# Second parts of weights on GpSimd during the expert choice, expert lists of 80 and 48 rows

## The chip, the cores and the metric

The kernel runs on one core of a Trainium2 chip. The metric is the device time of one execution in microseconds. The kernel before took 1815.71 us (median of three runs, 1813.82 to 1818.97).

## What is computed

Two encoder layers over 256 tokens of width 1024, all in float32. A layer is a mixer (one input projection, a neighbourhood attention, a sliding-window attention, gates, an output projection) and then a feed-forward part with retrieved experts, which is where the change lies:

```python
def peer_ffn(x, w_query, sub_keys, expert_down, expert_up):
    def chunk(xc):                                   # 128 tokens
        q = (xc @ w_query).reshape(PEER_CHUNK, PEER_HEADS, 2, half)
        s = jnp.einsum('thpk,pnk->thpn', q, sub_keys)
        sv, si = lax.top_k(s, PEER_TOPK)             # 16 of 128, twice a head
        cand = (sv[:, :, 0, :, None] + sv[:, :, 1, None, :]).reshape(...)
        cidx = (si[:, :, 0, :, None] * 128 + si[:, :, 1, None, :]).reshape(...)
        top_s, sel = lax.top_k(cand, PEER_TOPK)      # 16 of 256 pairs
        eidx = jnp.take_along_axis(cidx, sel, axis=-1)
        g = jax.nn.softmax(top_s, axis=-1)
        u, vv = expert_down[eidx], expert_up[eidx]   # 16384 experts
        act = gelu(jnp.einsum('td,thkd->thk', xc, u))
        return jnp.einsum('thk,thkd->td', (g * act), vv)
```

## The kernel before

**Number format.** Every float32 product is made of three matmuls: a weight is split into a first part `wh` (ScalarE, line 198) and a second part `wl = raw - wh` (VectorE, line 201), the left side likewise, and TensorE adds `h*h`, `h*l` and `l*h`. A unit of weights is 128 x 1024 values, 512 KB. The class `Stream` (lines 154 to 225) loads units on SyncE's queue some units ahead, splits them and hands them to TensorE; `splits` lists the names of the subtractions, in order.

**Stages of a layer.** Mixer; query projection, 16 units in four groups; then the *down stage*, 128 units: TensorE multiplies all 16384 rows of `peer_down` with all 256 tokens (lines 1363 to 1365, 24 matmuls a unit), and the result, after the gelu (line 1307), is `act`, 128 partitions x 128 rows i of experts x 256 tokens. Beside these matmuls runs the *expert choice*: scores (line 944), top 16 in eight groups n = 0 to 7 (`topk_lane`, lines 916 to 924 and the additions of line 964, all VectorE), indices and softmax (`index_lane`), and then 76 *gate groups* a layer (`gate_group`, lines 1065 to 1109), which multiply the gates into `act` in two passes: 44 groups for the rows 0 to 79 and 32 for the rows 80 to 127. A pass also counts which experts are used at all.

**Lists.** When a pass is through, `rank_lane` gives each expert of its list a place: first those that only the tokens of chunk 0 use, then those of both chunks, then those of chunk 1 alone. `send_lane` scatters the rows of `act` to these places in DRAM (line 1208, one indirect DMA a row of 128 experts, from GpSimd's queue). The *up stage* then reads a list back in blocks of 128 experts (line 1239, SyncE's queue), fetches the rows of `peer_up` that these experts name (line 1268, an indirect DMA of 512 KB from GpSimd's queue), splits them as units and multiplies (line 1397): a block costs six matmuls of 512 columns for each chunk that uses it. A list is a tuple (first row, rows, cap, ea, sb): the blocks sb to ea-1 are made for both chunks, 0 to sb-1 for chunk 0 alone, ea to cap-1 for chunk 1 alone. `WHOLE` names rows that are not sorted at all: their 128 experts are taken as they stand, for both chunks, their units loaded by plain DMAs on SyncE's queue, between the first list and the second. What the caps leave out would be made up by `make_up` behind a branch.

**Order and pace.** The order of instructions on each engine is fixed when the program is written out: `Lanes` keeps planned clocks (p TensorE, v VectorE, s ScalarE) and lets side lanes issue when their turn has come by planned costs. Waits between engines come from the data. A sending lane first needs its list's places (`lane_need([("rank", r)])`), then for each row that row's gelu and gates. Between sends it keeps a pace counted in weight splits: the counter starts three behind the splits written so far, each send adds 0.4 (first list) or, in the second list, 1.8 and later 0.6, and the send waits in the program and on the chip for the split that the counter names. The second list also waits until ten units of the up stage are loaded:

```python
            whole = up0 + len([x for x in seq if x[1] == 0])
            while r and st.nd < up0 + DEEP:
                yield None
            pace = len(st.splits) - 3.0
                pace += 0.4 if r == 0 else 1.8 if st.nd < whole else 0.6
```

`st.nd` counts the units loaded, `up0` is the first unit of the up stage. The reading back of a list starts only when all its rows are sent (line 1239 behind `sent`). Four units are loaded ahead; from the fourth unit before the up stage on, `st.depth` is ten, so that the split of the first up unit, written out two units before the end of the down stage, asks for units up to ten ahead.

Of the kernel before, what the change touches and what calls it, by code (L numbers as in the profile page):

```python
# [10 lines left out]
F32 = mybir.dt.float32  # L11
# [37 lines left out]

LISTS = [(0, 80, 66, 49, 16), (88, 40, 33, 25, 8)]  # L50
WHOLE = (80, 8)

# [18 lines left out]
class Lanes:  # L71
# [8 lines left out]
    def __init__(self):  # L80
        self.clk = {"p": 0.0, "v": 0.0, "s": 0.0}
        self.lanes = []
        self.stuck = 0
        self.urgent = 0
# [71 lines left out]
class Stream:  # L156


    def __init__(self, nc, pool, srcs, lanes):
        self.nc, self.pool, self.srcs, self.lanes = nc, pool, srcs, lanes  # L160
        self.raw, self.parts, self.ready = {}, {}, {}
        self.nd = self.np = self.want = 0
        self.ahead = self.depth = AHEAD
        self.busy, self.pooled, self.splits = set(), [], []
        self.rows = None
# [24 lines left out]
    def _prep(self, u):  # L190
        self.load(u)
        while u not in self.raw:
            yield None
            self.load(u)
        yield ("s", 0.97)
        r = self.raw.pop(u)
        h = self.pool.tile([128, UNIT], F32R, name="wh", bufs=AHEAD)
        self.nc.scalar.activation(h, r, AF.Copy)  # L198
        self.ready[u] = (yield ("v", 1.14)) - 0.05
        lo = self.pool.tile([128, UNIT], F32R, name="wl", bufs=AHEAD)  # L200
        self.splits.append(self.nc.vector.tensor_sub(lo, r, h.bitcast(F32)).ins.name)  # L201
        self.parts[u] = (h, lo)
        self.busy.discard(u)
        self.load(u + self.depth)
# [19 lines left out]
def encoder_kernel(ctx, tc, x_in, wts, downs, ups, gains, gate_bias, qk_norm, rpb, sink, skeys, consts, sums, out,  # L224
# [244 lines left out]
    u = 0  # L469
    acc_first = None  # L470

    for l in range(depth):
# [474 lines left out]
        def topk_lane():  # L947
            for n in range(8):
                cg, ch = n // 2, n % 2
                yield from lane_need([("s", cg, ch)])  # L950
                sc = area(4096 + n * 512, 512).rearrange("p (q n) -> p q n", n=128)
                s2 = area(8192 + (n % 2) * 512, 512).rearrange("p (q n) -> p q n", n=128)
# [238 lines left out]
        def send_lane(r):  # L1191

            i0, w = LISTS[r][:2]
            yield from lane_need([("rank", r)])
            whole = up0 + len([x for x in seq if x[1] == 0])
            while r and st.nd < up0 + DEEP:
                yield None
            pace = len(st.splits) - 3.0
            for i in range(i0, i0 + w):
# [17 lines left out]

                pace += 0.4 if r == 0 else 1.8 if st.nd < whole else 0.6
                sends[r].append(snd.ins)
# [350 lines left out]
```

## Time and profile before

| | us |
|---|---|
| median of the runs | 1815.71 |
| the profiled execution | 1816.92 |
| its span | 1815.1 |
| TensorE busy | 1777.3 (98%) |
| VectorE busy | 1452.2 (80%) |
| ScalarE busy | 1085.9 (60%) |
| GpSimd busy | 495.4 (27%) |

Both layers do the same work, the second some 901 us after the first. Times of a stage below are those of the first layer in the profiled execution; a busy TensorE means that a matmul was under way, and where matmuls are issued every 0.12 us (256 columns) or 0.23 us (512 columns) without a gap nothing holds TensorE back.

### The profile page before, as it was taken

To read this page: it belongs to the slowest core of one execution; us is meant where nothing else is said; L and a number is where in the kernel's file an instruction comes from. 1 tells how busy PE (TensorE), PEld (TensorE's weight loads), DVE (VectorE), ACT (ScalarE), POOL (GpSimd) and SP (SyncE) were. 2 spreads that over 40 slices of the span, in tenths; PEclk is the share of its full clock that TensorE was granted. 3 is DMA by queue.
4 is the path that set the end of the run, shared out by engine and by line. 5 is a ranking of instruction groups with operands and counts; after the bars stand their busy time and mean duration, and the time that the engine had idled before them with its cause. 6 is when DMAs were issued, how large, how long until landed. Compare 5 with 4: busy or idle time off the path is not lost. (4 is left out here: it accounts for less than half of the span.)

```text
span 1815.1 us, 38007 instructions
## 1 busy us (share of the span) xinstructions
PE 1777.3 (98%) x14646; PEld 1637.2 (90%) x14646; DVE 1452.2 (80%) x3270; ACT 1085.9 (60%) x1792; POOL 495.4 (27%) x448
## 2 busy tenths in 40 slices
PE   8999999999999989999999999999999999999998
PEld 7889899999999988878788998999999999888786
DVE  6986798988987877766689778989888878777665
ACT  5675555566656656665646654555665567566654
POOL 0000000000008767775200000000000187777661
PEclk9999999999999999999999999999999999999999
DMA  7535455544446869989564355555444478799893
GB/s 262 159 112 171 150 171 180 184 152 152 152 143 233 245 217 353 328 316 347 192 214 143 107 164 165 172 180 183 150 153 150 152 234 249 239 341 332 297 344 130
DMA packets 130519, 377.42 MB, mean 208 GB/s; under 512 B 17552, under 2 KB 43792, under 8 KB 130320
## 3 DMA queue, kind: packets, MB, share of 16 engines
q1 hardware_dynamic: 90288, 239.28, 42.5%
q0 software_dynamic: 40032, 135.54, 20.4%
q8 instruction: 119, 1.95, 0.4%
q14 instruction: 80, 0.66, 0.1%
HBM read 342.00 MB, written 32.75 MB: 206 GB/s over the span
## 5 line engine op out<-in xcount | busy, mean ns | idle before, releaser
L201 DVE TENSOR_TENSOR wl<-raw,wh 128x1024 fp32r<-128x1024 f32 x476 | 579.6, 1221 | 157.0 <-ACT wh L198 148.9
L198 ACT ACTIVATE wh<-raw 128x1024 fp32r<-128x1024 f32 x476 | 503.0, 1058 | 249.9 <-PE bank L1364 61.1
L1363 PE MATMUL bank<-TT,wh 128*128 128x256 f32 x2048 | 591.7, 289 | 0.0
L1364 PE MATMUL bank<-TT,wh 128*128 128x256 f32 x2048 | 578.9, 283 | 0.0
L1365 PE MATMUL bank<-TT,wl 128*128 128x256 f32 x2048 | 578.4, 282 | 0.0
L1364 PEld LDWEIGHTS bank<-TT,wh 128*128 128x128 f32 x2048 | 392.0, 191 | 0.0
L1365 PEld LDWEIGHTS bank<-TT,wl 128*128 128x128 f32 x2048 | 391.8, 191 | 0.0
L1363 PEld LDWEIGHTS bank<-TT,wh 128*128 128x128 f32 x2048 | 391.4, 191 | 0.0
L1397 PE MATMUL bank<-wh,TT 128*128 128x512 f32 x1296 | 350.2, 390 | 6.2 <-DVE TT L1286 2.2
L1208 POOL DMA_INDIRECT rows<-act,rank x240 | 280.4, 1168 | 96.3 <-issue 60.9
L1397 PEld LDWEIGHTS bank<-wh,TT 128*128 128x128 f32 x1296 | 242.2, 188 | 62.2 <-DVE TT L1286 5.4
L885 POOL IOTA act<- 128x128 uint32 (+2 forms) x6 | 2.0, 332 | 1081.1 <-PE bank L365 410.7
L201 DVE TENSOR_TENSOR wl<-act,wh 128x1024 fp32r<-128x1024 f32 x126 | 154.3, 1226 | 75.9 <-ACT wh L198 75.9
L1397 PE MATMUL bank<-wl,TT 128*128 128x512 f32 x648 | 200.6, 389 | 1.5 <-issue 1.5
L198 ACT ACTIVATE wh<-act 128x1024 fp32r<-128x1024 f32 x126 | 133.5, 1061 | 96.2 <-PE bank L1397 84.6
L1268 POOL DMA_INDIRECT act<-in_ups_dram,act x118 | 126.6, 1073 | 71.3 <-issue 30.2
L1397 PEld LDWEIGHTS bank<-wl,TT 128*128 128x128 f32 x648 | 121.6, 188 | 25.4
L445 PE MATMUL bank<-TT,wh 128*128 128x256 f32 x448 | 130.1, 290 | 1.6 <-ACT raw_ka L574 1.0
L447 PE MATMUL bank<-TT,wh 128*128 128x256 f32 x448 | 126.6, 283 | 0.0
L448 PE MATMUL bank<-TT,wl 128*128 128x256 f32 x448 | 126.6, 283 | 0.0
L1307 ACT ACTIVATE act<-bank 128x256 f32<-128x256 f32 (+9 forms) x216 | 66.1, 350 | 84.7 <-PE bank L1365 82.2
L1109 DVE TENSOR_TENSOR act<-act,bank 128x480 f32<-128x480 f32 (+32 forms) x152 | 71.3, 471 | 51.8 <-ACT act L1105 45.8
(267 smaller groups left out, 2852.1 us busy)
## 6 DMA issues: line engine op xcount, KB each, us to landing
raw<-in_downs_dram SPq DMA_DIRECT2D x256, 512.0 KB, 3.8
raw<-in_wts_dram SPq DMA_DIRECT2D x132, 512.0 KB, 4.2
act<-rows SPq DMA_DIRECT2D x100, 129.0 KB, 5.9
act<-rows SPq DMA_DIRECT2D x98, 64.5 KB, 5.2
act<-in_ups_dram SPq DMA_DIRECT2D x8, 512.0 KB, 8.9
raw<-in_ups_dram SPq DMA_DIRECT2D x8, 512.0 KB, 9.8
rows<-act,rank POOLq DMA_INDIRECT x240
act<-in_ups_dram,act POOLq DMA_INDIRECT x118
```

The costliest lines, as they stand in the source:

```text
L198: self.nc.scalar.activation(h, r, AF.Copy)
L201: self.splits.append(self.nc.vector.tensor_sub(lo, r, h.bitcast(F32)).ins.name)
L445: nc.tensor.matmul(o, wh, rh, start=first and i == 0 and pc == 0, stop=False, skip_group_check=True)
L447: nc.tensor.matmul(o, wh, rl, start=False, stop=False, skip_group_check=True)
L448: nc.tensor.matmul(o, wl, rh, start=False, stop=last and i == len(kcs) - 1 and pc == 1, skip_group_check=True)
L1109: nc.vector.tensor_mul(a, a, bv[:, 0:g])
L1208: snd = nc.gpsimd.indirect_dma_start(byrank[r], bass.IndirectOffsetOnAxis(ap=rank[:, i:i + 1], axis=0), afl[:, i * ROW:(i + 1) * ROW], None)
L1268: nc.gpsimd.indirect_dma_start(w, None, ups_rows, bass.IndirectOffsetOnAxis(ap=num, axis=0), element_offset=l * 16384 * D)
L1363: nc.tensor.matmul(o, lh, TT[:, :, 0, kc, :], start=kc == 0, stop=False)
L1364: nc.tensor.matmul(o, lh, TT[:, :, 1, kc, :], start=False, stop=False)
L1365: nc.tensor.matmul(o, ll, TT[:, :, 0, kc, :], start=False, stop=kc == 7)
L1397: nc.tensor.matmul(oacc[ch][hf], a, r[:, hf * 512:(hf + 1) * 512], start=first[hf] and a is lh and r is h, stop=last and a is ll)
```

## The change

Three edits. The lists become 80 and 48 rows: the second list takes over the eight rows that were whole, and its caps go from (33, 25, 8) to (40, 29, 9). While `topk_lane` is in its groups 0 to 6, the second part of each weight unit is subtracted by GpSimd instead of VectorE, with a planned clock g of its own. And the second list no longer waits for ten loaded up units: it is sent as soon as its places are known, behind the first list, at 0.4 a send until six up units are loaded and at 1.8 from there on.

```diff
-LISTS = [(0, 80, 66, 49, 16), (88, 40, 33, 25, 8)]
-WHOLE = (80, 8)
+LISTS = [(0, 80, 66, 49, 16), (80, 48, 40, 29, 9)]
+WHOLE = (80, 0)
...
-        self.clk = {"p": 0.0, "v": 0.0, "s": 0.0}
+        self.clk = {"p": 0.0, "v": 0.0, "s": 0.0, "g": 0.0}
...
+        self.gpsimd = False
...
         self.nc.scalar.activation(h, r, AF.Copy)
-        self.ready[u] = (yield ("v", 1.14)) - 0.05
+        engine, req = ((self.nc.vector, ("v", 1.14)), (self.nc.gpsimd, ("g", 2.5)))[self.gpsimd]
+        t = yield req
         lo = self.pool.tile([128, UNIT], F32R, name="wl", bufs=AHEAD)
-        self.splits.append(self.nc.vector.tensor_sub(lo, r, h.bitcast(F32)).ins.name)
+        self.splits.append(engine.tensor_sub(lo, r, h.bitcast(F32)).ins.name)
+        self.ready[u] = t - 0.05
...
                 yield from lane_need([("s", cg, ch)])
+                st.gpsimd = n < 7
...
             yield from lane_need([("rank", r)])
-            whole = up0 + len([x for x in seq if x[1] == 0])
-            while r and st.nd < up0 + DEEP:
-                yield None
             pace = len(st.splits) - 3.0
...
-                pace += 0.4 if r == 0 else 1.8 if st.nd < whole else 0.6
+                pace += 0.4 if r == 0 or st.nd < up0 + 6 else 1.8
```

## Rows read from the trace of the kernel before

**Rows 1.** the page, its head and part 1: TensorE
```profile
span 1815.1 us, 38007 instructions
...
PE 1777.3 (98%) x14646; PEld 1637.2 (90%) x14646; DVE 1452.2 (80%) x3270; ACT 1085.9 (60%) x1792; POOL 495.4 (27%) x448
```

**Rows 2.** stretches: PE, PEld, DVE, ACT, POOL busy, PEclk, DMA share, GB/s
```profile
210.70:303.50 92.80, 92.80 (x780) 92.80 (x779) 88.56 (x454) 45.09 (x62) 0.00 (x0) 1.00 0.54 169
...
362.00:536.00 174.00, 174.00 (x1950) 172.19 (x1949) 151.68 (x301) 107.78 (x192) 0.19 (x1) 1.00 0.48 151
536.00:671.50 135.50, 134.61 (x1717) 133.03 (x1716) 111.00 (x235) 90.17 (x149) 96.71 (x83) 1.00 0.69 215
671.50:684.50 13.00, 7.55 (x39) 5.32 (x38) 7.55 (x21) 5.78 (x9) 9.89 (x11) 0.74 1.03 388
684.50:772.00 87.50, 87.50 (x388) 72.47 (x388) 64.18 (x89) 57.46 (x87) 68.03 (x64) 1.00 0.99 338
```

**Rows 3.** VectorE groups, 210.7 to 303.5 us: count, busy us, mean ns, idle
```profile
L201 DVE TENSOR_TENSOR wl<-raw,wh 128x1024 fp32r<-128x1024 f32 x30 | 36.3, 1213 | 4.1 <-ACT wh L198 3.9
...
L964 DVE TENSOR_TENSOR act<-act 128x16 f32<-128x16 f32 (+3 forms) x40 | 4.3, 174 | 0.0
```

**Rows 4.** line 944, first layer: count, ns min/median/max, first and last start
```profile
L944 ACT ACTIVATE act<-bank x8: 599/599/602, 210.1 to 250.1; 128x512 f32<-128x512 f32 x8
```

**Rows 5.** GpSimd groups by form, whole span
```profile
L885 POOL IOTA act<- 128x128 uint32 x2 | 0.9, 436 | 410.7 <-PE bank L365 410.7
...
L885 POOL IOTA act<- 128x28 uint32 x2 | 0.4, 190 | 350.8 <-PE bank L1092 350.8
```

**Rows 6.** lines 1092 and 1174 in the first layer
```profile
L1092 PE MATMUL bank<-oh x384: 182/184/204, 368.3 to 668.1; 128*128 128x48 f16 x128, 128*128 128x80 f16 x64
...
L1092 PE MATMUL bank<-act x128: 197/200/204, 374.1 to 533.5; 128*128 128x80 f16 x128
...
L1174 DVE CAST rank<-scr x2: 202/256/309, 542.7 to 682.5; 128x80 uint32<-128x80 f32 x1, 128x40 uint32<-128x40 f32 x1
```

**Rows 7.** GpSimd's timeline, first layer: start us, duration us, operation, idle before
```profile
543.80 2.15 POOL L1208 DMA_INDIRECT rows<-act,rank  x1 [9.81 <-DVE miss L1180]
...
661.15 1.19 POOL L1208 DMA_INDIRECT rows<-act,rank  x1 [0.30 <-issue]
...
668.64 0.97 POOL L1268 DMA_INDIRECT raw<-in_ups_dram,act  x1 [6.30 <-DVE wh L1286]
...
693.68 1.15 POOL L1208 DMA_INDIRECT rows<-act,rank  x1 [0.30 <-issue]
...
798.43 0.99 POOL L1208 DMA_INDIRECT rows<-act,rank  x1 [0.30 <-issue]
```

**Rows 8.** TensorE's timeline where the up stage begins, first and second layer
```profile
671.72 0.28 PE L1365 MATMUL bank<-TT,wl 128*128 128x256 f32 x1
...
677.45 0.68 PE L1159 MATMUL bank<-scr 128*40 128x128 f16 x4 [5.45 <-DVE scr L1153]
...
684.49 0.18 PE L1184 MATMUL bank<-miss,scr 128*128 128x2 f16 x1
...
1573.45 0.28 PE L1365 MATMUL bank<-TT,wl 128*128 128x256 f32 x1
...
1585.38 0.18 PE L1184 MATMUL bank<-miss,scr 128*128 128x2 f16 x1
```

**Rows 9.** timelines of SyncE, ScalarE and VectorE at the same place, first layer
```profile
665.52 23.65 SPq L1239 DMA_DIRECT2D act<-rows  x21
...
674.05 1.06 ACT L198 ACTIVATE wh<-raw 128x1024 fp32r<-128x1024 f32 x1 [5.75 <-DMA raw<-in_ups_dram,act]
...
675.14 1.23 DVE L201 TENSOR_TENSOR wl<-raw,wh 128x1024 fp32r<-128x1024 f32 x1 [6.38 <-ACT wh L198]
```

**Rows 10.** line 1397: the blocks whose weights lie in wh, both layers
```profile
L1397 PE MATMUL bank<-wh x24: 388/395/797, 678.1 to 1585.1; 128*128 128x512 f32 x24
...
L1397 PE MATMUL bank<-wl,wh x12: 389/391/628, 679.1 to 1584.7; 128*128 128x512 f32 x12
```

## What I predict, and how it is worked out

> **What bounds the kernel now.** I read the page's head first, then the table of stretches, then the timelines around the one place where TensorE stops. TensorE is busy for 98% of the span [rows 1], and in the stretches of the expert choice (210.7 to 303.5 us), of the first gate pass (362 to 536) and of most of the up stage (684.5 to 772) it is busy all the time at the full granted clock [rows 2]. So the time is TensorE's work plus the stops between stages. A shorter side chain pays only where it ends such a stop, or where it lets TensorE do fewer matmuls. The largest stop inside a layer is where the up stage begins: of the 13.0 us from 671.5 to 684.5 TensorE is busy 7.55, and the granted clock falls to 0.74, that is, part of it runs at 1.2 instead of 2.4 GHz [rows 2].
>
> Behind this stop stands a chain which is not TensorE's. The first list's last send is issued at 661.15, the first read-back can only start at 665.52, the first fetch of `peer_up` rows at 668.64, ScalarE waits 5.75 us for that transfer until 674.05, and the first second part ends at 675.14 + 1.23 = 676.4 [rows 7, 9]. From the last send to the first usable unit: 15.2 us. The sends run from 543.80 to 661.15, 80 in 117.4 us, 1.49 us apart, with GpSimd never waiting long [rows 7]; they start where the first list's places are known, at 542.7 [rows 6]; and that moment is set by VectorE, through the choice and the gate groups: VectorE is busy 88.56 of 92.8 us in the choice and 151.68 of 174 us in the first gate pass [rows 2]. So VectorE's share of the choice sets when the sends are through.
>
> **Part 1, fewer blocks.** Work per chunk, before: first list 33 blocks for both chunks and 33 for one, 99; second list 17 for both and 16 for one, 50; eight whole rows, 16; together 165. After: 99 and, from 20 blocks for both and 20 for one, 60; together 159. Six chunk-blocks fewer a layer, of six matmuls each. A matmul costs 87.5/388 = 0.2255 us in the up stage [rows 2], a chunk-block 1.353 us: 8.1 us a layer, **16.2 us in all**, on the path, since nothing else fills TensorE there. Costs of this edit at nothing: seven more read-backs and fetches and eight more sends, less eight plain loads, a layer. They lie on SyncE's and GpSimd's queues, which are beside the path: GpSimd is busy 68.03 of 87.5 us in the up stage [rows 2]. The units per chunk-block hardly change (106 for 159 instead of 107 for 165), and DMA moved 338 GB/s in the up stage but 388 in the stop before it [rows 2], so there is room. If that room were not there, the loads would be the next thing late.
>
> **Part 2, second parts on GpSimd.** In the choice, VectorE spends 36.3 us on 30 subtractions of 1.213 us and waits 4.1 us for first parts [rows 3]. The eight groups therefore take 92.8 - 36.3 - 4.2 = 52.3 us of VectorE, 6.54 each. After: seven groups without subtractions, 45.8 us, and the eighth with them (a unit lasts 24 matmuls x 92.8/780 = 2.86 us [rows 2], of which 1.213 is the subtraction), 6.54/(1 - 1.213/2.86) = 11.4; together 57.2 instead of 92.8. The choice ends 35.6 us earlier, if its scores are there in time: group 6 starts at 210.7 + 6 x 6.54 = 250, and the last score tile is written at 250.1 [rows 4], so just so. About 16 units (45.8/2.86) go to GpSimd, which is idle in this stretch (POOL 0.00 [rows 2]).
>
> What GpSimd takes for such a subtraction no row shows. Its nearest rows are its iotas: 128 elements a partition in 436 ns, 28 in 190 [rows 5], so 2.46 ns an element and some 0.12 us more, which makes 2.64 us for 1024. From below, VectorE's 1.21 us; from above, twice the iota's for two operands read, 5.3 us. I take 2.64, the row of the same engine. As long as it is under the 2.86 us of a unit, four units loaded ahead cover it and TensorE sees nothing; over that, TensorE waits for the difference, 16 times a layer.
>
> The trace shows the additions of line 964 (two operands in SBUF, 40 in the choice, five a group) at 174 ns [rows 3], all of them while GpSimd is idle, so no row shows what they cost beside it. The Trainium skill (SBUF — State Buffer, Who interferes with whom) says that a VectorE instruction with two SBUF inputs and a GpSimd instruction that reads SBUF exclude each other, and that the later one waits for the whole of the other. By that rule each group of additions would wait for at least one GpSimd subtraction, which would take back up to 2.64 us in each of seven groups, 18 of the 35.6 us, and more if all five waited. No run here shows it so far. The maximum searches that make up most of the choice read one operand, and the rule would leave them alone.
>
> **Part 3, what an earlier choice moves.** Indices and gate groups are VectorE's too, so I let the 35.6 us pass through them. First list: places at 507 instead of 543, sends through at 626 instead of 661. The up units are first asked for some eight units ahead of the end of the down stage (four split ahead, four loaded ahead of the split), at 671.8 - 8 x 2.86 = 649, so they no longer wait for sends. The stop then goes. What it is worth: in the first layer the last down matmul is issued at 671.72, and the 18 early block matmuls (36 in both layers [rows 10]) and the ranking of the second list, all before 684.49 [rows 8], are worth 18 x 0.2255 + 0.6 = 4.7 us (0.6 for the ranking is my estimate of its 16 small matmuls), so of 12.77 us, less 0.12 for the down matmul itself, 8.0 are lost; in the second layer, from 1573.45 to 1585.38, 7.2 us. What stays I put at 1.3 us a layer: the ranking's waits move into the down stage (the stretch with the first ranking has 134.61 of 135.5 busy [rows 2]). **Gain 12.5 us in all**, 0 to 15.2 as the bounds.
>
> Second list: its last gate matmul is at 668.1 [rows 6]; the first list needed 542.7 - 533.5 = 9.2 us from its last one to its places, so without the stop the second's would be known at 677 (in the trace 682.5 [rows 6], behind the up stage's first splits). Less 35.6: 641.5. The fast pace holds until six up units are loaded, two units before the end of the down stage, 671.8 - 2 x 2.86 = 666.1: (666.1 - 641.5)/1.49 = 16.5 sends, and 3/1.8 = 1.7 more at once because the counter starts three behind. The other 29.8 go at the slow pace, 3.74 us apart (29 sends from 693.68 to 798.43 [rows 7]): through at 777.5. They are needed when? The up stage starts at 672.5, its first list takes 99 x 1.353 = 133.9 us, the second list's first block is due at 806.4 and takes 15.2 us from the last send, so 791.2. Covered by 14 us. That cover replaces the eight whole rows (16 x 1.353 = 21.6 us of work that needed no list), and it is thin: it is gone when the choice gains less than 30 us. On GpSimd's queue the early fetches now stand among fast sends, at most 1.49 us each, with four units of cover.
>
> **The sum.** 16.2 + 12.5 = 28.7 us. The profiled execution took 1816.92, span 1815.1 and 1.8 around it; 1816.9 - 28.7 = 1788.2. It stood 1.2 us over the median, so 1787.0.
>
> **Rivals.**
> *The second list comes late, slower.* Mechanism: the choice does not get shorter as VectorE's additions wait behind GpSimd's subtractions, or the gates do not follow it; then TensorE stands before block 66. It decides from an advance under 30 us. With half of it (17.8 us) the places are known at 659, 6.4 sends are early, 37.5 more go by 806.4, four more at 1.49 us bring 812.7, and the first block is there at 827.9: a stop of 21.5 us a layer against 8.1 + 6.3 gained, 1816.9 + 14.2 - 1.2 = 1830. With no advance the old stop stays too and the sum is some 1866. For it: nothing whole is left to cover; 14 us is a small margin on numbers from one trace. Against: VectorE has idle time in the gate stretches (22 of 174 us [rows 2]) in which it can catch up lost time, as the order on it is planned with the earlier end. The rule of the Trainium skill (SBUF — State Buffer, Who interferes with whom) gives this result if all additions wait.
> *GpSimd is slower than a unit.* At 5.3 us TensorE would wait 16 x 2.4 = 39 us a layer: 1865. It decides from 2.86 us.
> *Only the blocks count.* The stop at the start of the up stage has another cause next in line (the last gelu's bank, the ranking, the first split): 1816.9 - 16.2 - 1.2 = 1799.5. A list late by a few us falls here too.
> *Nothing to measure.* An advance of 25 us: places at 652, 11 sends early, the last at 804, a stop of 13 us a layer, 1787 + 26 = 1813.
>
> **How the numbers follow.** A measurement of this kernel can tell about 0.3%, 5.4 us, from no change. Forecast (1778 to 1798) 0.60; only the blocks, or a small stop (1798 to 1810) 0.15; nothing to measure 0.08; second list late 0.12; GpSimd too slow 0.05. So faster 0.75, same 0.08, slower 0.17. The range runs from 1777 (the whole stop gone, a little less idle at the end of the first list) to 1812 and leaves out both slower rivals and a little below.
>
> **What would show it.** Right: GpSimd rows of line 201 with a mean between 2.2 and 2.86 us; line 916's last start some 35 us earlier than before; the first send at about 508; line 1397's first start within 2 us of the last down matmul, at a granted clock of 1.00 throughout; some 1908 matmuls on line 1397 instead of 1980; the second list's last send before 791, with no stop of TensorE before block 66. Wrong: additions of line 964 behind GpSimd, a stop of TensorE at about 806, or gaps of TensorE between 210 and 260.

## The result, and the profile after

The changed kernel takes 1833.74 us (median of six runs, 1830.08 to 1836.23); the kernel before, beside it, 1815.6. The ratio is 1.0092, 95% interval 1.0079 to 1.0105: slower by 18 us, where the prediction said 28.7 us faster. The profiled execution has a span of 1830.0, 14.9 more than that of before. The experiments ran on other chips, on four of the five of which the kernel before itself takes 1940 to 1958 us and on the fifth 1818, so every experiment is given as a ratio to the kernel before on its own chip.

The page's head and its line of TensorE, of after (they answer [rows 1]): TensorE has as much to do as before, 2.3 us more by its busy time, and 15 us more span.

```profile
span 1830.0 us, 37960 instructions
...
PE 1779.6 (97%) x14574; PEld 1621.0 (89%) x14574; DVE 1436.8 (79%) x3274; ACT 1092.4 (60%) x1784; POOL 629.5 (34%) x510
```

**The choice became shorter, as meant.** The groups of GpSimd and VectorE in the choice of after, 210.7 to 277.5 us (columns as in [rows 3]):

```profile
L203 POOL TENSOR_TENSOR wl<-raw,wh 128x1024 fp32r<-128x1024 f32 x16 | 38.5, 2413 | 27.7 <-ACT wh L199 27.7
...
L968 DVE TENSOR_TENSOR act<-act 128x16 f32<-128x16 f32 (+3 forms) x40 | 13.0, 389 | 0.0
```

GpSimd makes 16 second parts at 2.41 us; the prediction estimated 2.64. VectorE's additions take 389 ns instead of the 174 of [rows 3], 8.7 us more in all. The search for the largest ends 24 us earlier (the last one starts at 277.1 instead of 301.2).

**The sends moved with it.** The line that writes the places, of after, first layer (it answers the last row of [rows 6]): 25.6 us earlier for the first list, 39.8 for the second.

```profile
L1178 DVE CAST rank<-scr x2: 190/196/203, 517.1 to 642.7; 128x80 uint32<-128x80 f32 x1, 128x48 uint32<-128x48 f32 x1
```

**The stop at the start of the up stage moved, and then the whole stage ran short.** TensorE's timeline of after where the up stage begins (it answers [rows 8]): the first block follows 0.1 us behind the last matmul of the down stage at 674.06, and the 18 matmuls that stood around the old stop are through at 678.51 (before at 684.49 [rows 8]). TensorE stops some 8 us into the stage instead, for 4.96 us in the first layer and 6.69 in the second, where the old stops cost 8.0 and 7.2.

```profile
674.06 0.28 PE L1366 MATMUL bank<-TT,wl 128*128 128x256 f32 x1
674.18 0.63 PE L1398 MATMUL bank<-wh 128*128 128x512 f32 x2
...
678.51 0.62 PE L1398 MATMUL bank<-wh,TT 128*128 128x512 f32 x2
...
682.13 0.61 PE L1398 MATMUL bank<-wh,TT 128*128 128x512 f32 x2
687.71 1.12 PE L1398 MATMUL bank<-wh,TT 128*128 128x512 f32 x2 [4.96 <-ACT TT L1285]
...
1597.08 1.22 PE L1398 MATMUL bank<-wh,TT 128*128 128x512 f32 x2 [6.69 <-ACT TT L1285]
```

Stretches of after in the up stage (columns as in [rows 2]):

```profile
684.00:704.00 20.00, 16.30 (x64) 13.17 (x65) 11.69 (x15) 10.82 (x16) 16.04 (x14) 0.91 0.91 296
700.00:720.00 20.00, 19.58 (x81) 14.16 (x80) 12.37 (x17) 11.63 (x18) 15.92 (x14) 1.00 0.93 304
...
780.00:800.00 20.00, 18.88 (x75) 13.54 (x76) 13.33 (x18) 10.89 (x19) 16.04 (x14) 1.00 0.91 294
...
820.00:840.00 20.00, 20.00 (x89) 16.50 (x88) 15.39 (x21) 13.63 (x22) 12.93 (x12) 1.00 1.04 395
```

and of before, which [rows 2] shows only as one long stretch:

```profile
700.00:720.00 20.00, 20.00 (x90) 16.53 (x89) 14.49 (x20) 12.92 (x20) 15.43 (x16) 1.00 0.99 327
...
780.00:800.00 20.00, 20.00 (x89) 16.55 (x89) 14.21 (x20) 12.38 (x20) 15.43 (x16) 1.00 0.95 323
```

The matmul counts are the reading that matters: 90 in 20 us is the full rate. From 684 to 820 after has 64 to 82, and the busy share hides it, since a matmul that waits a little is still under way. The granted clock is 1.00 in all of these rows but the first (0.91), so it is not the clock. From 820 on, when the fetches of the first list are through, the rate is full again. The DMA engines move less in these rows (294 to 304 GB/s instead of 323 to 327), and moved 395 from 820 to 840. What TensorE lacked is seen one step back, in ScalarE's waits, after (674 to 910 us: us in total, times, longest):

```profile
ACT wh L199 <- DMA act<-in_ups_dram,act: 36.0, 26, 5.7
...
ACT wh L199 <- DMA raw<-in_ups_dram,act: 20.5, 18, 2.5
```

and before (684 to 910 us), where ScalarE waits for TensorE to free a buffer:

```profile
ACT wh L198 <- PE bank L1397: 70.7, 54, 1.5
ACT wh L198 <- DMA act<-in_ups_dram,act: 3.3, 2, 2.1
```

**The queue that issues the fetches.** GpSimd's timeline of after (it answers [rows 7]):

```profile
633.23 0.96 POOL L1209 DMA_INDIRECT rows<-act,rank  x1 [0.30 <-issue]
643.71 1.91 POOL L1209 DMA_INDIRECT rows<-act,rank  x1 [9.52 <-ACT wh L199]
...
660.63 0.97 POOL L1269 DMA_INDIRECT raw<-in_ups_dram,act  x1 [2.10 <-DVE wl L203]
661.91 1.13 POOL L1209 DMA_INDIRECT rows<-act,rank  x1 [0.30 <-issue]
...
804.64 0.99 POOL L1209 DMA_INDIRECT rows<-act,rank  x1 [0.30 <-issue]
...
814.84 0.94 POOL L1269 DMA_INDIRECT act<-in_ups_dram,act  x1 [0.30 <-issue]
```

The first list's 66th and last fetch is issued at 814.84. Before it was this row:

```profile
799.73 1.14 POOL L1268 DMA_INDIRECT act<-in_ups_dram,act  x1 [0.30 <-issue]
```

From the first fetch to that row the queue never waits for anything worth naming in either kernel: 0.30 us between two instructions, nearly always. So the time of the 66th fetch can be taken apart. Before: 97 instructions (66 fetches, 31 sends) in 131.1 us, 1.366 each. After: 105 (66 and 39) in 154.2 us, 1.483 each. It starts 8.0 us earlier, has eight more sends (8 x 1.366 = 10.9), and each of the 104 steps is 0.117 us longer (12.2): -8.0 + 10.9 + 12.2 = 15.1 us later. The blocks that remain are fewer by what Part 1 said, 8.1 us. That leaves 7.0 us a layer. This is a sum of readings of two traces; no run changed one of its terms alone. It fits the rest: the choice of the second layer starts 6.3 us later than before, and the span is 14.9 us longer.

### The profile page after: what moved, and what is told of

Its sections match the earlier page's. It is cut to its first block, busy times and chain, and to the rows that moved or that the text cites. A ratio compares the mean times of both kernels' runs of the same rounds, so it can differ in the third digit from the quotient of the medians.

```text
span 1830.0 us, 37960 instructions
## 1 busy us (share of the span) xinstructions
PE 1779.6 (97%) x14574; PEld 1621.0 (89%) x14574; DVE 1436.8 (79%) x3274; ACT 1092.4 (60%) x1784; POOL 629.5 (34%) x510
## 5 line engine op out<-in xcount | busy, mean ns | idle before, releaser
L203 DVE TENSOR_TENSOR wl<-raw,wh 128x1024 fp32r<-128x1024 f32 x444 | 541.6, 1222 | 144.6 <-ACT wh L199 140.8
L1209 POOL DMA_INDIRECT rows<-act,rank x256 | 300.5, 1174 | 119.7 <-issue 58.5
L1398 PEld LDWEIGHTS bank<-wh,TT 128*128 128x128 f32 x1248 | 230.8, 190 | 103.5 <-ACT TT L1285 31.5
L1398 PE MATMUL bank<-wl,TT 128*128 128x512 f32 x624 | 195.9, 394 | 0.0
L1269 POOL DMA_INDIRECT act<-in_ups_dram,act x124 | 146.2, 1179 | 73.7 <-DVE TT L1287 36.5
L1269 POOL DMA_INDIRECT raw<-in_ups_dram,act x88 | 103.6, 1177 | 47.7 <-issue 18.3
L1072 ACT ACTIVATE oh<-oh 128x1024 f16<-128x1024 f16 (+2 forms) x108 | 101.4, 955 | 11.4 <-DVE oh L1069 10.4
```

The costliest lines, as they stand in the source:

```text
L203: self.splits.append(engine.tensor_sub(lo, r, h.bitcast(F32)).ins.name)
L1072: nc.scalar.activation(el, ej, AF.Copy, scale=LOW)
L1209: snd = nc.gpsimd.indirect_dma_start(byrank[r], bass.IndirectOffsetOnAxis(ap=rank[:, i:i + 1], axis=0), afl[:, i * ROW:(i + 1) * ROW], None)
L1269: nc.gpsimd.indirect_dma_start(w, None, ups_rows, bass.IndirectOffsetOnAxis(ap=num, axis=0), element_offset=l * 16384 * D)
L1398: nc.tensor.matmul(oacc[ch][hf], a, r[:, hf * 512:(hf + 1) * 512], start=first[hf] and a is lh and r is h, stop=last and a is ll)
```

## The experiments

The theories, as the expectations name them. *Queue*: GpSimd's queue of sends and fetches is full in the up stage and sets the end of the first list. *Transfer*: the moved bytes set it. *Order*: it is only that sends stand ahead of the first fetches. *Stage*: the loss lies in the choice and the gates. *Lock*: VectorE's instructions with two operands in SBUF hold up GpSimd's issues, that is, its sends and fetches.

**GpSimd's second parts alone** (three runs of the same kernel: the kernel before plus the change's edits for line 201):

```diff
-        self.ready[u] = (yield ("v", 1.14)) - 0.05
+        engine, req = ((self.nc.vector, ("v", 1.14)), (self.nc.gpsimd, ("g", 2.5)))[self.gpsimd]
+        t = yield req
...
+                st.gpsimd = n < 7
```

> The kernel before with the subtraction on GpSimd during the choice and nothing else of the change. Queue theory (the up stage of the changed kernel is slow because GpSimd's queue, one instruction after another, cannot issue the sends and fetches at TensorE's pace, and the early sends took the place of the first fetches): the earlier choice removes the stop of 8.0 and 7.2 us at the start of the up stage, and as the second list still waits for ten loaded units, the fetches come first; 1815.6 less 10 to 15: 1801 to 1806. Rival, the subtraction on GpSimd is itself what costs (additions blocked, TensorE waiting in the choice): 1815 or more.

> The same kernel as the first one of the call before (before with the subtraction on GpSimd alone), since the kernel before itself took 7% longer on that chip, with waits that its first profile does not have. Queue theory on a chip where the kernel before takes about 1815: 1801 to 1806. Rival, GpSimd's subtraction is what costs: 1815 or more.

> The kernel before with the second parts on GpSimd during the choice and nothing else. By the prediction's third part the stop at the start of the up stage goes, 10 to 15 us: 1801 to 1806. Queue theory: the end of the first list is set by the fetches and the sends among them, which start no sooner than some eight units ahead of the up stage; the time that the stop costs TensorE is the time in which the queue gets its lead, so most of it is lost again: 1808 to 1822, ratio 0.996 to 1.004. Where the kernel before takes 1940 us it gave 1.001 and 1.002.

Measured: 1.0012 (0.9978 to 1.0046), 1.002 (0.9997 to 1.0044), 1.002 (0.9986 to 1.0053). The first send moves from 543 to 518 us, as in the changed kernel, and nothing comes of it. But these runs can't say what the stop of Part 3 was worth, since on these chips there is next to no such stop to remove. No profile of the kernel before was taken there, but in the runs below that leave its choice as it was the blocks follow the down stage almost at once. In one of them (three iotas behind every fourth fetch, see below), TensorE's last down matmul, first block matmul and 19th are:

```profile
723.96 0.28 PE L1368 MATMUL bank<-TT,wl 128*128 128x256 f32 x1
...
725.74 0.73 PE L1400 MATMUL bank<-wh 128*128 128x512 f32 x2
...
730.65 0.71 PE L1400 MATMUL bank<-wh,TT 128*128 128x512 f32 x2
```

That is 6.7 us, against 12.8 in the trace of before [rows 8]. With GpSimd's second parts, on the same chip, it is 15.1 us:

```profile
716.39 0.28 PE L1369 MATMUL bank<-TT,wl 128*128 128x256 f32 x1
...
727.33 0.77 PE L1401 MATMUL bank<-wh 128*128 128x512 f32 x1 [7.90 <-DVE act L1317]
...
731.49 0.62 PE L1401 MATMUL bank<-wh,TT 128*128 128x512 f32 x2
```

So here the second parts alone bring a stop instead of removing one. From the first fetch of the list to the 66th the queue issues one instruction in 1.59 to 1.63 us (98 instructions), with seven or eight waits of over 0.4 us in between, 16 to 22 us in all.

**The lists alone** (the changed kernel without its second parts on GpSimd):

```diff
-                st.gpsimd = n < 7
```

> The changed kernel with all subtractions on VectorE: new lists, second list behind the first. Queue theory: the first list is through at 662 as before, the second list's places come some 35 us later than in the changed kernel, nearly all its 48 sends fall into the up stage, the stop at the start stays; 1850 to 1870. Rival, that the lists and their order cost nothing by themselves and GpSimd's subtractions cause the loss: about 1800 (six chunk-blocks a layer fewer).

Measured: 1.0177 (1.0131 to 1.0222). The second parts alone cost nothing clear of noise, the lists with their early sending cost 1.8%.

**The old lists with the early sending** (the changed kernel with the lists of before):

```diff
-LISTS = [(0, 80, 66, 49, 16), (80, 48, 40, 29, 9)]
-WHOLE = (80, 0)
+LISTS = [(0, 80, 66, 49, 16), (88, 40, 33, 25, 8)]
+WHOLE = (80, 8)
```

> The changed kernel with the lists of the kernel before (80 rows, 40 rows, eight whole rows) and the new order of sends: second list right behind the first. Queue theory: the first fetches still come behind fast sends, so a stop of some 5 us at the start stays, and the loss at 2.2 us a unit until the sends are through; but eight sends and seven fetches fewer stand before the second list's blocks and 21.6 us of whole rows cover it; 1810 to 1830, slower than the subtraction on GpSimd alone by 8 to 25 us. Rival, the lists' sizes are what costs and the order is harmless: as the subtraction on GpSimd alone, 1801 to 1806.

Measured: 1.0047 (1.0028 to 1.0066), about as the changed kernel in the next run.

**The changed kernel again, and with the second list's sends held from the first up unit until ten are loaded, and then paced at 1.2 splits:**

```diff
             for i in range(i0, i0 + w):
+                while r and up0 < st.nd < up0 + DEEP:
+                    yield None
...
-                pace += 0.4 if r == 0 or st.nd < up0 + 6 else 1.8
+                pace += 0.4 if r == 0 or st.nd < up0 + 6 else 1.2
```

> The changed kernel itself, unaltered, beside the variants of it: where the kernel before takes 1939.7 us as in the two calls before, GpSimd's sends and fetches are slower against TensorE, so the queue theory wants a larger loss than the 0.9% first measured: 1.01 to 1.03 of the kernel before (1960 to 2000). The reference for every third block loaded plainly (0.984 of the kernel before).

> The changed kernel, but the second list's sends pause from the first up unit's fetch until ten units are loaded, and then keep a pace of 1.2 splits instead of 1.8, so that the list is in time. Order theory (the loss is that fast sends stood before the first fetches): the gain that was forecast comes back, 28 us or more under the changed kernel. Queue theory: the same 114 sends and fetches stand before the second list, only in another order; the stop of 5 us at the start goes and comes back before the second list; within 10 us of the changed kernel.

Measured: 1.0061 (1.0033 to 1.0089) and 1.0038 (1.0007 to 1.0069). The same within their intervals, though the order did change: behind the first fetch come nine sends and then eleven fetches in a row, where the changed kernel has a mixture. On these chips the order of sends and fetches on the queue is not the cause.

**Sixteen whole rows** (the second parts on GpSimd, the second list with eight sends and six fetches less and eight plain units more than before):

```diff
-LISTS = [(0, 80, 66, 49, 16), (88, 40, 33, 25, 8)]
-WHOLE = (80, 8)
+LISTS = [(0, 80, 66, 49, 16), (96, 32, 27, 20, 6)]
+WHOLE = (80, 16)
```

> The subtraction on GpSimd alone, with sixteen whole rows instead of eight (lists of 80 and 32 rows): eight sends and six fetches fewer a layer on GpSimd's queue, seven chunk-blocks more a layer on TensorE (9.5 us). Queue theory: GpSimd's 14 instructions of 1.3 to 1.5 us, 18 to 21 us a layer, are worth more than TensorE's 9.5, so 10 to 20 us under the subtraction alone (1944.8 where it was measured). Transfer theory: 19 us over it, since the bytes stay and the matmuls grow.

Measured: 1.0124 (1.0092 to 1.0155). The queue theory as I had put it fell here. Eight whole rows more are 16 chunk-blocks, while the shorter list has nine fewer (41 instead of 50): seven more at 1.353 us are 9.5 us a layer, 19 in all, and that is what this run costs over the second parts alone (0.0112 x 1941 = 22). The fourteen instructions less on GpSimd's queue gave nothing there.

**Every third fetch of the first list as a plain load** (22 a layer, from SyncE's queue; the loaded rows are not the ones that the list names). Three runs on the changed kernel, two on the kernel before:

```diff
-            if w is not None and r is None:
+            if w is not None and (r is None or r == 0 and k % 3 == 2):
```

> The changed kernel, but every third block of the first list loads 512 KB of peer_up by a plain DMA on SyncE's queue in place of the indirect one on GpSimd's (other rows than the list names, so the output is not the reference's); the same bytes and the same matmuls. Queue theory: 22 of the 114 sends and fetches leave GpSimd's queue ahead of the second list, some 30 us a layer, more than the 22 us that the up stage lost; 1785 to 1800. Transfer theory (the DMA engines cannot move sends, read-backs and fetches together at TensorE's pace): no change, 1830 to 1836.

> The changed kernel with every third block of the first list loaded by a plain DMA of the same size (other rows than the list names, so the output is not the reference's), repeated for the same reason; the changed kernel itself took 1833.7. Queue theory: 1785 to 1800, with TensorE's matmuls 0.2255 us apart from 690 us on. Transfer theory: 1830 to 1836.

> The changed kernel with every third fetch of the first list (22 of 66 a layer) replaced by a plain load of the same size from SyncE's queue, so it multiplies other rows than the list names. On the chips of the runs so far, where the kernel before takes some 1940 us, this gave 0.983 and 0.984. What is open is what it gives where the kernel before takes 1815 us. Queue theory: the up stage of the changed kernel is held back by GpSimd's queue, at some 1.4 us an instruction; 22 instructions fewer free 31 us a layer, more than the 22 us that TensorE loses there, so the up stage runs at its full rate from its start and the sum of the prediction comes out: 1785 to 1800, ratio 0.983 to 0.992. Transfer theory (the same bytes on the same DMA engines): within 6 us of the changed kernel's 1834. Stage theory (the loss lies in the choice and the gates): 1820 or more.

> The kernel before with every third block of the first list loaded by a plain DMA of the same size (other rows than the list names, so the output is not the reference's). With GpSimd's queue relieved in both kernels, the changed one should be under this one by what the prediction's sum gives, 20 to 30 us, if the sum was right and only the queue was left out; so 1930 to 1940 against 1907 for the changed kernel with the same loads. If the sum itself was wrong, the two are within 10 us.

> The kernel before with the same 22 plain loads a layer in place of fetches, so it multiplies other rows than the list names. Queue theory, where the kernel before takes 1815 us: TensorE loses only some 2 to 4 us a layer in its up stage, and the stop at its start is not the fetches', so it gains 3 to 10 us: 1805 to 1812, ratio 0.994 to 0.998. Where the kernel before takes 1940 us it gave 0.977. The difference between this run and the changed kernel with the same plain loads is what the change is worth with the queue relieved: 10 to 25 us by the sum of the prediction, nothing if the sum was wrong elsewhere too.

Measured on the changed kernel: 0.9832 (0.9806 to 0.9858), 0.9842 (0.9823 to 0.9862), 0.9831 (0.9764 to 0.9898). On the kernel before: 0.9769 (0.9735 to 0.9804), 0.978 (0.9707 to 0.9852). The same stretch of the up stage in the changed kernel, without and then with plain loads (on two of these chips; columns as in [rows 2]):

```profile
740.00:820.00 80.00, 70.67 (x290) 55.49 (x290) 47.62 (x64) 42.30 (x64) 55.21 (x51) 0.96 0.86 275
```

```profile
740.00:820.00 80.00, 78.88 (x347) 64.69 (x346) 56.23 (x77) 50.33 (x78) 55.38 (x48) 1.00 0.98 341
```

With the fetches taken off the queue TensorE gets 347 matmuls instead of 290 in 80 us, and the DMA engines carry 341 GB/s instead of 275, with the same units to load: the engines had room. But the kernel before gains as much, so on these chips it is held up by its fetches as well, and the changed kernel with plain loads is not faster than the kernel before with them: 0.6% slower on the chip that ran both. The rows show where that lies. The last down matmul, the first matmul behind the stop and the 19th block matmul, changed kernel with plain loads:

```profile
717.43 0.28 PE L1366 MATMUL bank<-TT,wl 128*128 128x256 f32 x1
...
735.97 0.76 PE L1398 MATMUL bank<-wh 128*128 128x512 f32 x1 [16.64 <-DVE act L1314]
...
740.79 1.05 PE L1398 MATMUL bank<-wh,TT 128*128 128x512 f32 x2
```

and the kernel before with them, on the same chip:

```profile
727.73 0.28 PE L1365 MATMUL bank<-TT,wl 128*128 128x256 f32 x1
...
733.36 0.70 PE L1397 MATMUL bank<-wh,TT 128*128 128x512 f32 x2
```

From the last down matmul to the 19th of the blocks it is 23.4 us instead of 5.6, and in the second layer 24.0 instead of 5.6. From there to the end of the up stage the changed kernel is the shorter one, by 5.6 us in the first layer and 7.7 in the second, against Part 1's 8.1. So with the queue relieved the fewer blocks are nearly worth what was predicted, and a stop at the start of the up stage, which the kernel before doesn't have on these chips, takes more than that back. What TensorE waits for in this stop was not traced further.

**More work for GpSimd, no more transfers** (the kernel before with small iotas behind fetches): one behind each fetch, three behind each (this is the edit shown), three behind every fourth of the first list.

```diff
+    spare = cpool.tile([128, 128], U32, name="spare")
...
+                for _ in range(3):
+                    nc.gpsimd.iota(spare, pattern=[[1, 128]], base=0, channel_multiplier=0)
```

> The kernel before with one more GpSimd instruction, an iota of 128 elements (0.44 us and the 0.3 us between instructions at most), behind each indirect fetch; its result is not used. Queue theory: GpSimd is near its limit in the up stage already, 66 x 0.45 to 0.75 us a layer less the cover that the loaded units give: 1840 to 1900. Transfer theory: GpSimd has room, 1815 to 1820.

> The kernel before with three more iotas of 128 elements behind each indirect fetch (0.25 us each and about 0.15 between them, 1.2 us a fetch; results not used). Queue theory: with 1.3 us for each send and fetch and 0.56 sends a unit GpSimd's queue needs 2.0 us a unit before and 3.2 with the iotas, against TensorE's 2.03; 66 blocks of the first list and 33 of the second, 60 to 100 us a layer, 1930 to 2010. Transfer theory: GpSimd's time is hidden, 1815 to 1825.

> The kernel before, with three small iotas of GpSimd ahead of every fourth fetch of the first list: 17 places a layer, some 1.2 us each, 20 us of GpSimd's queue a layer and no transfer, about what the change's eight further sends and seven further fetches add. Queue theory: GpSimd's queue is full in the up stage of the kernel before as well (16 instructions per 20 us), so these 20 us come back as 10 to 20 us a layer: 1835 to 1855, ratio 1.011 to 1.022. Transfer theory: nothing, within 5 us. An iota ahead of every fetch (some 60 us a layer, gaps included) cost nothing where the kernel before takes 1940 us, three of them cost 53 us a layer; so there it should cost nothing.

Measured: 0.9989 (0.9959 to 1.002), 1.0577 (1.0539 to 1.0616) and 0.9952 (0.9918 to 0.9986). An iota takes 0.24 us, but one behind a fetch puts off the next instruction by only 0.12 us, since 0.30 us pass there anyway: some 12 us a layer. Three put it off by 0.8 to 1.2 us: up to 20 us a layer at 17 places, up to 117 at 99. The heavy load costs 53 us a layer; the two light ones cost nothing. The queue's timeline shows the slack that took them: between the first and the 66th fetch it waits eight times for over 0.4 us with one iota behind each fetch, 15 us in all. So these runs, on chips where the queue waits, don't carry over as a price per instruction.

**What stretches an issue.** In the kernel before, 0 of 73 issues between 690 and 790 us take 1.3 us or more (mean 1.05); in the changed kernel 19 of 66 between 700 and 800 (mean 1.20). Into the kernel before, I put one more VectorE instruction ahead of the second part of every third up unit: once the same subtraction, with two operands, once a multiplication by 1, with one. Both write a value that the subtraction then overwrites.

```diff
+        if isinstance(self.srcs[u], tuple) and u % 3 == 0:
+            self.nc.vector.tensor_sub(lo, r, h.bitcast(F32))
```

```diff
+        if isinstance(self.srcs[u], tuple) and u % 3 == 0:
+            self.nc.vector.tensor_scalar(lo, r, 1.0, None, op0=OP.mult)
```

> The kernel before; in the up stage every third unit's second part is computed twice by VectorE, so one more instruction of 1.22 us with two operands in SBUF every 6.1 us. Lock theory: a send or a fetch of GpSimd that meets such an instruction stretches; the share of issues of 1.3 us and more, 10 of 64 in the run with GpSimd's second parts alone (740 to 840 us), rises by 5 to 12 of 64, and the mean from 1.12 to 1.2 or more. Rival (the transfers stretch the issues): mean and share stay, within 3 of 64. Time: by the lock theory 0 to 20 us longer, by the rival within 6 us.

> The same place, but the additional VectorE instruction is a multiplication by 1 with one operand in SBUF. Lock theory: no more long issues than without it (7 to 12 of 64), mean 1.09 to 1.14. If any VectorE work stretched the issues, this run would show as many long ones as the other.

Measured, on the chip where the kernel before takes 1817.56: two operands 1.0051 (1.0034 to 1.0068), 9 us; one operand 1.0182 (1.0165 to 1.0199), 33 us. Long issues between 740 and 840: 4 of 66 and 25 of 60, against 4 of 65 in the kernel before, all four behind 800. That is the reverse of what I expected. Stretches of the run with one operand:

```profile
700.00:720.00 20.00, 20.00 (x90) 16.55 (x89) 16.90 (x24) 12.73 (x21) 16.04 (x14) 1.00 0.95 297
720.00:740.00 20.00, 20.00 (x90) 16.56 (x89) 15.17 (x22) 11.76 (x19) 16.19 (x13) 1.00 0.90 286
740.00:760.00 20.00, 19.59 (x78) 13.43 (x77) 13.58 (x19) 10.16 (x16) 16.19 (x13) 1.00 0.91 286
760.00:780.00 20.00, 18.08 (x66) 12.91 (x67) 12.90 (x18) 10.62 (x17) 16.34 (x13) 0.91 0.83 263
```

and of the run with two:

```profile
740.00:760.00 20.00, 20.00 (x90) 16.53 (x90) 17.63 (x24) 12.84 (x20) 15.43 (x16) 1.00 0.96 329
```

The run with one operand loses TensorE's rate as the changed kernel does, with no send and no fetch added, and the run with two, which gives VectorE more work, does not. It also gives the order of events: from 700 to 740 GpSimd already issues 13 or 14 in 20 us instead of 15 or 16, while TensorE still runs at 90, out of its lead. TensorE falls short from 740. So in this run the slow issues come first, and the starved TensorE behind them. The 66th fetch is issued at 817.53 instead of 799.73, 17.8 us later (97 instructions at 1.557 us); the kernel is 33 us longer in two layers, 16.7 each. In the run with two operands it is issued at 801.64.

Why one and not the other is seen in single issues. GpSimd's rows of the kernel before, and behind the dots VectorE's at the same place (start us, duration us, operation):

```profile
725.02 0.99 POOL L1208 DMA_INDIRECT rows<-act,rank  x1 [0.30 <-issue]
726.32 1.11 POOL L1268 DMA_INDIRECT raw<-in_ups_dram,act  x1 [0.30 <-issue]
727.73 1.04 POOL L1268 DMA_INDIRECT raw<-in_ups_dram,act  x1 [0.30 <-issue]
...
725.37 1.23 DVE L201 TENSOR_TENSOR wl<-act,wh 128x1024 fp32r<-128x1024 f32 x1 [1.16 <-ACT wh L198]
...
726.73 1.23 DVE L201 TENSOR_TENSOR wl<-act,wh 128x1024 fp32r<-128x1024 f32 x1
...
729.45 1.23 DVE L201 TENSOR_TENSOR wl<-act,wh 128x1024 fp32r<-128x1024 f32 x1 [1.16 <-ACT wh L198]
```

The same of the changed kernel, three issues and the subtractions that they begin in:

```profile
710.11 1.44 POOL L1269 DMA_INDIRECT act<-in_ups_dram,act  x1 [0.31 <-issue]
...
721.93 1.61 POOL L1269 DMA_INDIRECT raw<-in_ups_dram,act  x1 [0.31 <-issue]
...
729.11 1.89 POOL L1209 DMA_INDIRECT rows<-act,rank  x1 [0.30 <-DMA act<-rows]
...
709.49 1.23 DVE L203 TENSOR_TENSOR wl<-act,wh 128x1024 fp32r<-128x1024 f32 x1 [0.57 <-ACT wh L199]
...
721.49 1.23 DVE L203 TENSOR_TENSOR wl<-raw,wh 128x1024 fp32r<-128x1024 f32 x1 [0.41 <-ACT wh L199]
...
728.89 1.23 DVE L203 TENSOR_TENSOR wl<-raw,wh 128x1024 fp32r<-128x1024 f32 x1 [0.71 <-ACT wh L199]
```

The subtraction from 721.49 ends at 722.72, the issue that began inside it at 723.54, 0.82 us later; the other two pairs give 0.83 and 0.88. One rule fits most of them, sends and fetches alike: an issue that begins inside a subtraction of VectorE ends 0.80 to 0.95 us after that subtraction. Before, 690 to 790 us, it holds for 49 of 49; after, 690 to 800, for 42 of 45; in the run with two operands, 690 to 790, for 65 of 65, in the one with one operand for 28 of 40. Of the exceptions ten end 1.03 to 1.17 us after the subtraction. Five begin in its first 0.03 us and are not held at all; in these the subtraction takes 1.26 to 1.29 us instead of 1.23. An issue that begins outside takes 0.94 to 1.00 us before (24 issues). So an issue is held until the subtraction is through and then needs some 0.84 us. How long it is held depends on where in the subtraction it begins. In the kernel before, it always begins 0.18 to 0.35 us ahead of the end: TensorE frees a buffer pair every 4.08 us, ScalarE and VectorE follow in a fixed rhythm, and three issues (0.99, 1.11, 1.04 and three times 0.30) make 4.04 of these 4.08 us. In the changed kernel they begin 0.03 to 1.12 us ahead of it, since ScalarE, and VectorE behind it, often wait there for a fetch to land (ScalarE's waits above) and have no such rhythm. The inserted instruction with one operand breaks the rhythm as well (0.01 to 1.13 us), the one with two operands hardly (0.08 to 0.96, mean 0.24). Nearly all of the held issues stand in subtractions, which have two operands, in both runs. But that two operands are needed is not shown: two issues began inside the one-operand instruction, and they end 0.83 and 0.86 us after it; and six of the issues that end later than the rule says end 0.12 us after such an instruction, which began 0.25 us behind the subtraction.

The Trainium skill (SBUF — State Buffer, Who interferes with whom) says that a VectorE instruction with two SBUF inputs and a GpSimd instruction that reads SBUF exclude each other. The traces agree one way: these sends and fetches read their places from SBUF, and a subtraction holds them. The other way they show little of it: in the kernel before 49 subtractions begin 0.30 us or more behind the start of an issue that is still under way, and all take their 1.22 to 1.23 us.

## Why the prediction was wrong

**Part 1** had the blocks right: the matmuls of the up stage are 1908 over the two layers, the count that was predicted, and the pair with plain loads shows nearly their price. The step that failed is the sentence that put the further sends and fetches at nothing because GpSimd's queue is "beside the path: GpSimd is busy 68.03 of 87.5 us in the up stage". The same row [rows 2] says 64 instructions, and [rows 7] shows 0.30 us ahead of each: 64 x 0.30 = 19.2, and 68.03 + 19.2 = 87.2 of 87.5 us. The queue was full and just kept up with TensorE. The prediction named the condition, "the loads would be the next thing late", and looked for it in the DMA engines' room, where there was room, instead of in the queue that feeds them.

**Part 2** was nearly right. The subtraction takes 2.41 us for an estimated 2.64, TensorE sees nothing of it (66.80 busy of 66.80 us in the choice), and the rule of the Trainium skill (SBUF — State Buffer, Who interferes with whom) that was weighed there is seen: five additions from 215.12 on that meet GpSimd's subtractions take 3.66 us. It took back 8.7 us of the 35.6; 24 came through to the end of the choice (the other 3 us are not accounted for), and 25.6 to the places of the first list, so the first send stood at 517.6 instead of the predicted 508.

**Part 3** had the size of the stop right and its worth wrong. From the last down matmul to the end of the 18 early block matmuls it is 4.5 us instead of 12.8, so the up stage had its start 6.0 us earlier (the down stage itself ended 2.3 us later, at 674.06 instead of 671.72). But in the old stop the queue went on: before, 13 fetches had been issued by 684.5; after, eight by that time, and four when the up stage began at 674.2. The stop was the time in which the lead was made. Without it TensorE ran out of units and stopped some 8 us into the stage, for 5.0 and 6.7 us, and the 66th fetch came 15.1 us later than before. The step that failed here is that the stop was counted as a gain with no look at what sets the end of the first list. That the term of 12.5 us is worth nothing is read from this trace; the second parts alone don't test it, as their chips have no such stop.

**The second list** was sent through at 804.6, not 777.5, because each send stood in the full queue. It was needed at 791 by the prediction's count. By then TensorE was so far behind that it didn't wait for it long: there is no stop of the kind the slower rival describes at 806, only the rate that is short from 684 on. So the slower rival's 1830 came near the measured time by luck, as the mechanism is not the one that it describes: not one list that is late, but a fetch that is late for nearly every unit.

**The sum, put right.** With the queue as the bound the working is: 8.0 us earlier start, eight more sends at 1.366, fewer blocks: -8.0 + 10.9 - 8.1 = -5.2 us a layer, 10 us faster. What turned it into 15 us slower is the 0.117 us by which each issue became longer once the rhythm was lost, 12.2 us a layer; the prediction had no term for it. That a lost rhythm does this to the queue is shown by the run with one operand; the split into 10.9 and 12.2 is worked out from two traces, and no run tested it. The size could not be read from the trace before, but that the issues there stood in step with VectorE could.

**Open.** Whether the changed kernel can be kept in step was not tried on a chip like the first; holding its second list's sends until ten units were loaded was tried only where the queue of every run waits in between. Why these four chips take 1940 us and more is not known. Which of two things broke the rhythm, the early start with four units or the sends among the first fetches, isn't told apart. No version of the change here beats the kernel before.

## What to carry to other kernels

An engine that issues transfers is full when its busy time plus the gap ahead of each instruction fills the stretch; count instructions, not busy share. Before a stop is counted as a gain, look at which queue runs on during it: if that queue sets the end of the stage, the stop may be free. And count matmuls per stretch: TensorE busy for 19.58 of 20 us ran 81 matmuls here instead of 90.

## What was not expected of the hardware

An indirect transfer issued by GpSimd that begins inside a VectorE subtraction is held until that ends and then takes some 0.84 us more (up to 2.0 us in all instead of 0.94 to 1.00); in the kernel before this held for 49 of 49. So the rate of GpSimd's queue depends on the phase between the two engines: 1.37 us an issue in step, 1.48 to 1.56 out of step. One VectorE instruction of 0.69 us in every third unit was enough to lose the step, 33 us; a longer one of 1.22 us was not, 9 us. VectorE's additions, in turn, wait for GpSimd's subtractions: 389 ns instead of 174.
